# Where an RWKV step prepares its second unit and scales its output, and which loads an attention phase issues first

## The chip, the cores and the metric

The kernel runs on one core of a Trainium2 chip, as one program with one launch. The metric is device time in microseconds (us), the median of several runs; lower is better. The engines are TensorE (PE, with its weight loads PEld), VectorE (DVE), ScalarE (ACT), GpSimd (POOL) and SyncE (SP), which issues nearly all DMAs. Each engine takes its instructions in the order in which the program lists them, and waits at the first one whose inputs or buffers are not ready.

## The reference

One hybrid layer over 2048 tokens of width 1024, in float32. Cut to what matters here:

```python
p = rmsnorm(x, norm_g) @ w_in                  # 3076 columns, split into the parts below
# RWKV branch, 8 heads of 64, a recurrence over tokens:
S = S*w_t + sa*(kk_t*a_t) + v_t*k_t            # sa = S @ (-kk_t)
y = S @ r_t
y = (y - mean)*rsqrt(var + 64e-5)*gn_g + gn_b  # per head
y = y + sum(r*k*r_k)*v;  y = y*silu(gate)
# attention branch, 8 heads: every query picks its best 256 keys by an index score,
# softmax over them, then o * silu(gate)
out = rmsnorm(x + concat(y_rwkv, y_attn) @ w_out, final_g)
```

## The kernel before, in words

There are four phases. `phase_as` makes the projections and, for each of the 16 blocks of 128 queries, a mask of the chosen keys (`d_mask`). `phase_r` is the RWKV recurrence. `phase_t` is the attention with those masks, in 64 units: a unit (p, b) is head pair p of 4 and query block b of 16, with b the inner loop, so a unit costs more the larger b is. `phase_w` is the output product, one block of 128 tokens at a time; a block needs the RWKV output and all four head pairs' attention output of its tokens.

The phases are not run one after the other. A planner orders each engine's instructions ahead of time, on a timeline of its own. Among the instructions that are ready on this timeline the one with the lowest priority number goes first. Numbers rise in the order in which the code is written, and `later(n)` adds n millions: RWKV's state chain has no addition, the work around it has one (`e.later()`), attention two, the output product three. So attention fills the places that RWKV leaves. The order that comes out is fixed; on the chip an instruction that is not ready holds up all that stand behind it on its engine. `tc.issue_after(ins)` (in the code also `behind(ins)`) adds that the instructions of a block which run on the engine of `ins` stand behind it.

`phase_r` takes 16 steps n of 128 tokens. Each step has two units (i = 0, 1; each holds two of the four pairs of heads) and two chunks of 64 tokens (o = 0, 1). The functions:

- `prep(n, i)` loads a unit (`ld`, two buffers), makes decays, keys and the matrix `E` on DVE, ACT and PE, and `bv`. It ends with a scaling of `BK` on POOL, which stands behind the last instruction of the inverse that was traced before it (`scaled_after`).
- `systems` sends four pieces of `E` to memory (`du`, L1015) and reads them back spread over 128 partitions as `A` (L1017). `A` has one buffer, so its read can only start when the inverse before has read the last of the old `A`.
- `inverse` is 62 small POOL instructions in a row (L1031, L1033); its result goes out as `dx` (L1034) and comes back as `TT` (four DMAs, L1038).
- `prep2` transposes a unit's keys and values.
- `chain(n, o)` runs one chunk through the state: products, a solve with `TT` in two halves (first `TT` product L1068), and the new state `S` by two adds on DVE (L1096). What it returns as `state` is the last of them.
- `tail_norm` makes mean and variance of a step's output `y` on DVE and ACT, the power -0.5 on POOL (`gst`, L1112, behind the inverse's last instruction) and the scaling of `y` on DVE (L1113). `tail_out` transposes `y`, applies gains, `bv` and the gate (POOL, L1128 and L1129), and stores it.

At step n the code opens with inverse(n+1), then `tail_norm` of step n-1 with the scaling as its last instruction, then prep(n+2, 0) behind the last state. After chain(n, 0) come `prep2` of step n+1, prep(n+2, 1) behind the state of chain(n, 0), and `systems` for n+2. After chain(n, 1) comes `tail_out` of step n-1.

In `phase_t`, `load(p, b)` issues a unit's DMAs on SP: keys `kt` and values every fourth unit, queries `q` every second, mask `mk` and gate `ga` always. The first unit is loaded ahead of the loop; in turn i the loop loads unit i+1.

Of the kernel before, what the change touches and what calls it, by code (L numbers as in the profile page):

```python
# [14 lines left out]
OP = mybir.AluOpType  # L15
# [871 lines left out]
def phase_r(env):  # L887


    e = NS(env)  # L890
    nc, tc, pa, ps, dma, V, S, G, PE, f32, rpow, nm, ident = (
        e.nc, e.tc, e.pr, e.psr, e.dma, e.V, e.S, e.G, e.PE, e.f32, e.rpow, e.nm, e.ident)
# [3 lines left out]
    NU = 2 * NC  # L896
# [203 lines left out]
    def tail_norm(y):  # L1100

        yv = y.rearrange("t c (h i) -> t (c h) i", h=2)
        st = tl([128, 3, NU], F32, "gst", 2)
        V.tensor_reduce(st[:, 0], yv, axis=AX.X, op=OP.add)
        V.tensor_scalar(st[:, 0], st[:, 0], 1.0 / 64, None, op0=OP.mult)
        bc = lambda a: a[:, :, None].to_broadcast([128, NU, 64])
        V.tensor_tensor(yv, yv, bc(st[:, 0]), op=OP.subtract)
        sq = tl([128, NU, 64], F32, "ysq")
        S.activation(sq, yv, AF.Square)
        V.tensor_reduce(st[:, 1], sq, axis=AX.X, op=OP.add)  # L1110
        V.tensor_scalar(st[:, 1], st[:, 1], 1.0 / 64, 64e-5, op0=OP.mult, op1=OP.add)
        m = G.tensor_tensor(st[:, 2], st[:, 1], e.mhalf[:, :NU], op=OP.pow)  # L1112
        V.tensor_tensor(yv, yv, bc(st[:, 2]), op=OP.mult)  # L1113
        return m.ins

    def tail_out(us, y):

# [20 lines left out]
    def behind(ins):  # L1138
        return tc.issue_after(ins) if ins else ExitStack()
# [7 lines left out]
    first = G.memset(eLs[0][:, :, 0:1], 1.0).ins  # L1147
# [10 lines left out]
    y0, b0, state = None, None, None  # L1158
    for n in range(N):
        b = batch.pop(n)  # L1160
        new = batch[n + 2] = begin(n + 2) if n + 2 < N else None
        nx = batch.get(n + 1)
        with e.later():
            if nx:
                nx.TT, first = inverse(nx.A)
            if b0:
                with behind(first):
                    tail_norm(y0)
            if new:
                with behind(state):  # L1170
                    new.us.append(prep(n + 2, 0, new.eC, first))
        y = tl([128, NC, 128], F32, "y", 2)
        state = chain(b.us, b.TT, b.eC, y, n, 0)
        with e.later():
            if nx:
                for u in nx.us:
                    prep2(u)
            if new:
                with behind(state):
                    new.us.append(prep(n + 2, 1, new.eC, first))  # L1180
                new.A = systems(new.us)
        state = chain(b.us, b.TT, b.eC, y, n, 1)
        with e.later():
            if b0:
                tail_out(b0.us, y0)
        y0, b0 = y, b
    with e.later():
        tail_norm(y0)
        tail_out(b0.us, y0)


def phase_t(env):

    e = NS(env)
# [124 lines left out]

    units = [(p, b) for p in range(NP) for b in range(NB)]  # L1320
    last, stores, marks = None, [], {}
    load(*units[0])
    for i, u in enumerate(units + [None]):
        out = []
        ready, stores = stores, []
        if i + 1 < len(units):
            with tc.issue_after(load(*units[i + 1])):
                for x in ready:
                    dma(*x)
        else:  # L1330
            for x in ready:
                dma(*x)
        parts = [scores(*u, out)] if u else []
        if last:
            parts.append(attend(*last))
        while parts:
            parts = [g for g in parts if next(g, parts) is not parts]
        last = (*u, *out) if u else None
# [81 lines left out]
```

## Time and profile before

| | us |
|---|---|
| median of three runs (lowest, highest) | 2103.36 (2098.55, 2105.53) |
| the profiled execution, device time | 2104.7 |
| its span, first to last instruction | 2102.9 |
| PE busy in the span | 1803.3 (86%) |
| DVE, ACT, POOL busy | 1296.7, 1019.8, 795.3 |

The mean granted TensorE clock of the execution is 0.906 of full speed. RWKV's loads begin at 981 us; until then the span belongs to `phase_as`. The inverses run from 1025 to 1731 us, RWKV's last output is made at about 1800 us, and the last attention product ends at 2045 us. A busy share is an average over a stage; which wait ends last in a stage is read from the waits and the timeline.

### The profile page before, as it was taken

Reading aid. Unit: us, or ns where it says so; the run is one execution under the profiler, and the core shown is the slowest. Engines: PE = TensorE matmul, PEld = TensorE weight load, DVE = VectorE, ACT = ScalarE, POOL = GpSimd, SP = SyncE. Lnnn points to the kernel's source line nnn. Section 1 sums busy time; section 2 is a strip of 40 time slices with the busy share of each in tenths; the row PEclk is TensorE's granted clock in tenths of the full one; section 3 lists DMA queues with packets and bytes.
Section 4 is the critical chain, followed back from the end, with each engine's and each line's share of the span. In section 5 each row is a group of like instructions: output and inputs, shape, how many; then the busy total and the mean of one; then the engine's idle time right before and its main releaser. Section 6 shows DMA issues by size and latency. Waiting matters only on the chain.

```text
span 2102.9 us, 36153 instructions
## 1 busy us (share of the span) xinstructions
PE 1803.3 (86%) x12906; PEld 1421.8 (68%) x12906; DVE 1296.7 (62%) x3050; ACT 1019.8 (48%) x1966; POOL 795.3 (38%) x1925
## 2 busy tenths in 40 slices
PE   5788998879796988986788988886988889899998
PEld 4666877658575867765566766665766667587776
DVE  5532538979779698986656557564756654644432
ACT  4422494453444744441355555454655567643431
POOL 1110124353544354562445645654546650100000
PEclk9778999989798999998799998798988899999999
DMA  7526334332262434234844355343454324744223
GB/s 248 199 94 200 108 101 135 101 115 85 75 239 63 135 107 136 91 95 125 204 102 105 95 136 147 105 119 98 115 143 131 93 78 108 233 128 128 66 93 112
DMA packets 309038, 262.50 MB, mean 125 GB/s; under 512 B 82544, under 2 KB 258288, under 8 KB 307696
## 3 DMA queue, kind: packets, MB, share of 16 engines
q1 hardware_dynamic: 304464, 248.03, 40.1%
q0 software_dynamic: 4384, 12.06, 1.8%
q8 instruction: 104, 1.70, 0.4%
q14 instruction: 86, 0.70, 0.1%
HBM read 166.37 MB, written 97.85 MB: 126 GB/s over the span
## 4 chain that ended last, share of the span: by engine, by line
PE 23%; POOL 14%; DMA 12%; issue 5%; DVE 4%; SPq 1%; ACT 1%; POOLq 0%; DVEq 0%; ACTq 0%
DMA A<-du 6%; POOL Xr L1033 6%; POOL Xtmp L1031 5%; PE om L1304 3%; PE po L1381 3%; PE po L1382 3%; PE po L1384 3%; PE tr L1295 3%; DMA dx<-Xr 2%; PE s L1261 2%; PE s L1262 1%; DMA TT<-dx 1%; DMA ld<-d_rw 1%; POOL yo L1129 1%; POOL gst L1112 1%
## 5 line engine op out<-in xcount | busy, mean ns | idle before, releaser
L577 PE MATMUL pm<-xh,wh 128*128 128x512 f32 x800 | 330.4, 414 | 20.3 <-DVE t L588 11.8
L578 PE MATMUL pm<-xl,wh 128*128 128x512 f32 x800 | 327.0, 409 | 0.0
L579 PE MATMUL pm<-xh,wl 128*128 128x512 f32 x800 | 326.1, 408 | 0.0
L1263 DVE CUSTOM_DVE_ANT_0 sc<-s,mk 128x512 f32<-128x512 f32 (+3 forms) x320 | 187.9, 607 | 102.8 <-PE s L1262 76.0
L1297 ACT ACTIVATE pt<-tr 128x512 f32<-128x512 f32 (+1 forms) x288 | 157.9, 569 | 160.8 <-PE tr L1295 115.9
L1031 POOL TENSOR_TENSOR Xtmp<-Xr,A 128x60 f32<-128x60 f32 (+24 forms) x496 | 146.9, 296 | 225.8 <-DMA A<-du 181.8
L577 PEld LDWEIGHTS pm<-xh,wh 128*128 128x128 f32 x800 | 158.1, 198 | 61.7 <-DVE t L588 13.7
L1270 ACT ACTIVATE sc<-sc,mx 128x128 f32<-128x128 f32 (+15 forms) x128 | 153.0, 1198 | 63.0 <-DVE mx L1269 62.7
L1295 PE MATMUL tr<-ident,sc 128*128 128x128 f32 x1088 | 180.1, 292 | 3.0 <-ACT pt L1297 2.6
L579 PEld LDWEIGHTS pm<-xh,wl 128*128 128x128 f32 x800 | 157.3, 197 | 36.4
L578 PEld LDWEIGHTS pm<-xl,wh 128*128 128x128 f32 x800 | 158.0, 197 | 35.4
L1304 PE MATMUL om<-pt,vt 128*64 128x128 f32 x2176 | 174.0, 295 | 6.2 <-DVE ga L1287 6.2
L1261 PE MATMUL s<-kt,q 128*128 128x512 f32 (+2 forms) x320 | 144.2, 454 | 35.8 <-DVE mx L1263 32.2
L1033 POOL TENSOR_TENSOR Xr<-Xr,Xtmp 128x60 f32<-128x60 f32 (+24 forms) x496 | 151.3, 305 | 37.4
L1304 PEld LDWEIGHTS om<-pt,vt 128*64 128x64 f32 x2176 | 134.2, 146 | 37.6 <-issue 19.6
L1295 PEld LDWEIGHTS tr<-ident,sc 128*128 128x128 f32 x1088 | 133.5, 149 | 33.9 <-issue 11.4
L317 ACT ACTIVATE mk<-x,st 128x1920 bf16<-128x1920 f16 (+5 forms) x72 | 98.0, 1361 | 103.6 <-POOL st L314 103.6
L249 ACT ACTIVATE rl<-lg,wi 128x512 f32<-128x512 f32 (+3 forms) x152 | 94.0, 631 | 99.6 <-PE lg L247 53.1
L1262 PE MATMUL s<-kt,q 128*128 128x512 f32 (+2 forms) x320 | 123.3, 389 | 8.1 <-DMA q<-d_q 8.0
L320 DVE TENSOR_SCALAR_CACHE_REDUCE mk<-x,st 128x2048 bf16<-128x2048 f16 (+5 forms) x72 | 120.6, 1675 | 1.4
L254 DVE SCALAR_TENSOR_TENSOR xs<-rl,wi,xs 128x512 f32<-128x512 f32 (+3 forms) x108 | 73.5, 681 | 60.9 <-ACT rl L249 60.1
L1387 POOL TENSOR_TENSOR st<-st 128x1 f32<-128x1 f32 x16 | 3.1, 195 | 277.1 <-ACT po L1386 277.1
(329 smaller groups left out, 3937.7 us busy)
## 6 DMA issues: line engine op xcount, KB each, us to landing
wraw<-in_w_in_dram SPq DMA_DIRECT2D x42, 512.0 KB
d_rw<-t SPq DMA_DIRECT2D x80, 256.0 KB
ld<-d_rw SPq DMA_DIRECT2D x32, 640.0 KB
q<-d_q SPq DMA_DIRECT2D x128, 128.0 KB
d_q<-t SPq DMA_DIRECT2D x32, 256.0 KB
d_kt<-t SPq DMA_DIRECT2D x32, 256.0 KB
kt<-d_kt SPq DMA_DIRECT2D x32, 256.0 KB
A<-du SPq DMA_DIRECT2D x16, 512.0 KB
```

What stands on the lines that cost most here:

```text
L577: PE.matmul(pm, wh[:, k], XH[g][:, k], start=k == 0, stop=False)
L578: PE.matmul(pm, wh[:, k], XL[g][:, k], start=False, stop=False)
L579: PE.matmul(pm, wl[:, k], XH[g][:, k], start=False, stop=k == KD - 1)
L1031: G.tensor_tensor(tmp[:, :m, :w], Xr[:, :m, s:s + 1].to_broadcast([128, m, w]), A[:, s:s + 1, s + 1:].to_broadcast([128, m, w]), op=OP.mult)
L1033: m_ = G.tensor_tensor(Xr[:, :m, s + 1:], Xr[:, :m, s + 1:], tmp[:, :m, :w], op=OP.add)
L1261: PE.matmul(pS[:, :wp], qh[:, h, qs], k[:, h, :wp], start=True, stop=False)
L1262: PE.matmul(pS[:, :wp], ql[:, h, qs], k[:, h, :wp], start=False, stop=True)
L1263: V.tensor_tensor_reduce(out=rows[h][:, c0:c0 + w], in0=pS[:, :w], in1=mk[:, c0:c0 + w], scale=1.0, scalar=LOW, op0=OP.add, op1=OP.max, ac ...
L1270: marks[p, b] = S.activation(rows[h][:, :n], rows[h][:, :n], AF.Exp, bias=mx[:, h, 4:5], accum_out=sums[:, h:h + 1]).ins
L1295: PE.transpose(pt[:, i, h], rows[h][:, (kb + i) * 128:(kb + i) * 128 + 128], ident)
L1297: S.activation(w[:, :m], pt[:, :m], AF.Copy)
L1304: PE.matmul(po[HALF[h]], v[:, (kb + i) % 4, HALF[h]], w[:, i, h], start=kb + i == 0, stop=kb + i == b)
```

## The change

`prep` of both units and `systems` for step n+2 move to the opening of step n. `tail_norm` ends with the power and returns the scaling of `y`, which is traced after chain(n, 0) and behind its state. In `phase_t` the first three units are loaded before the loop, at a priority one million ahead of everything without an addition; the loop's loads begin with the fourth unit.

```diff
         V.tensor_scalar(st[:, 1], st[:, 1], 1.0 / 64, 64e-5, op0=OP.mult, op1=OP.add)
-        m = G.tensor_tensor(st[:, 2], st[:, 1], e.mhalf[:, :NU], op=OP.pow)
-        V.tensor_tensor(yv, yv, bc(st[:, 2]), op=OP.mult)
-        return m.ins
+        rpow(st[:, 2], st[:, 1])
+        return lambda: V.tensor_tensor(yv, yv, bc(st[:, 2]), op=OP.mult)
...
             if b0:
                 with behind(first):
-                    tail_norm(y0)
+                    scale = tail_norm(y0)
             if new:
-                with behind(state):
-                    new.us.append(prep(n + 2, 0, new.eC, first))
+                for i in range(2):
+                    with behind(state):
+                        new.us.append(prep(n + 2, i, new.eC, first))
+                new.A = systems(new.us)
         y = tl([128, NC, 128], F32, "y", 2)
         state = chain(b.us, b.TT, b.eC, y, n, 0)
         with e.later():
+            if b0:
+                with behind(state):
+                    scale()
             if nx:
                 for u in nx.us:
                     prep2(u)
-            if new:
-                with behind(state):
-                    new.us.append(prep(n + 2, 1, new.eC, first))
-                new.A = systems(new.us)
         state = chain(b.us, b.TT, b.eC, y, n, 1)
...
-        tail_norm(y0)
+        tail_norm(y0)()
         tail_out(b0.us, y0)
...
-    load(*units[0])
+    with e.later(-3):
+        for u in units[:3]:
+            load(*u)
     for i, u in enumerate(units + [None]):
         out = []
         ready, stores = stores, []
-        if i + 1 < len(units):
+        if 3 <= i + 1 < len(units):
             with tc.issue_after(load(*units[i + 1])):
```

`rpow` (L130) is the same POOL power as before, written as a helper.

## Rows read from the trace of the kernel before

**Rows 1.** Stretches: us, busy (count) of PE, PEld, DVE, ACT, POOL; clock, DMA, GB/s.
```profile
979.00:997.40 18.40, 3.91 (x25) 2.79 (x24) 13.53 (x40) 3.40 (x8) 4.03 (x17) 0.59 0.96 243
1025.00:1800.00 775.00, 660.15 (x7439) 511.48 (x7441) 448.22 (x1407) 431.30 (x989) 411.30 (x1177) 0.89 0.45 117
1800.00:1900.00 100.00, 90.55 (x568) 71.60 (x568) 49.37 (x128) 47.62 (x93) 3.26 (x10) 0.95 0.54 172
```

**Rows 2.** Waits of PE, 1025 to 1800 us: us in total, times, longest.
```profile
PE s L1261 <- DVE mx L1263: 32.2, 15, 7.0
PE ch L1068 <- DMA TT<-dx: 29.0, 5, 8.4
PE ch L1051 <- DVE S L1096: 14.4, 1, 14.4
PE rp L982 <- DVE E L977: 11.6, 2, 6.7
PE s L1262 <- DMA q<-d_q: 8.0, 1, 8.0
PE ch L1120 <- DVE S L1096: 7.8, 2, 4.3
PE rp L1051 <- DVE E L977: 4.8, 1, 4.8
...
PE rp L996 <- DVE bv L984: 4.4, 3, 1.7
```

**Rows 3.** Waits of DVE, the same stretch.
```profile
DVE y L1113 <- POOL gst L1112: 74.0, 11, 15.6
```

**Rows 4.** Timeline of DVE in one step: start, us, instruction, idle before and releaser.
```profile
1225.43 1.52 DVE L1113 TENSOR_TENSOR y<-y,gst 128x512 f32<-128x512 f32 x1 [5.60 <-POOL gst L1112]
...
1232.78 1.29 DVE L977 TENSOR_TENSOR E<-rp,mask 128x512 f32<-128x512 f32 x2 [1.38 <-PE rp L974]
```

**Rows 5.** Timeline of PE: two of its waits behind DVE.
```profile
1138.26 0.79 PE L1261 MATMUL s<-kt,q 128*128 128x512 f32 x1 [7.00 <-DVE mx L1263]
...
1733.63 0.58 PE L1261 MATMUL s<-kt,q 128*128 128x256 f32 x1 [6.75 <-DVE mx L1263]
```

**Rows 6.** Timeline of POOL: end of one inverse to start of the next, twice.
```profile
1223.74 1.66 POOL L1112 TENSOR_TENSOR gst<-gst,mhalf 128x8 f32<-128x8 f32 x1
...
1250.71 0.24 POOL L1031 TENSOR_TENSOR Xtmp<-Xr,A 128x31 f32<-128x31 f32 x1 [16.65 <-DMA A<-du]
...
1322.82 1.66 POOL L1112 TENSOR_TENSOR gst<-gst,mhalf 128x8 f32<-128x8 f32 x1
...
1338.06 0.24 POOL L1031 TENSOR_TENSOR Xtmp<-Xr,A 128x31 f32<-128x31 f32 x1 [7.98 <-DMA A<-du]
```

**Rows 7.** Timeline of SP's issues in the same two turns.
```profile
1237.71 0.55 SPq L1017 DMA_DIRECT2D A<-du  x1
...
1325.86 0.83 SPq L1017 DMA_DIRECT2D A<-du  x1
1327.69 1.89 SPq L1038 DMA_DIRECT2D TT<-dx  x4
```

**Rows 8.** Turns with A issued early (first, last, their sum of four), then ten others' sum.
```profile
1322.90:1363.40 40.50, 33.23 (x340) 26.90 (x338) 23.52 (x66) 17.93 (x43) 26.35 (x75) 0.75 0.41 106
...
1644.30:1687.30 43.00, 34.64 (x389) 26.93 (x388) 24.55 (x77) 24.09 (x53) 25.94 (x75) 0.88 0.39 101
sum 168.30, PE 135.67 PEld 108.06 DVE 97.36 ACT 85.83 POOL 104.39; mean PE 33.92 PEld 27.01 DVE 24.34 ACT 21.46 POOL 26.10
...
sum 471.30, PE 407.06 PEld 314.30 DVE 281.38 ACT 268.71 POOL 253.21; mean PE 40.71 PEld 31.43 DVE 28.14 ACT 26.87 POOL 25.32
```

**Rows 9.** Chain of waits that ended last: start, us, what.
```profile
1608.81 10.17 DMA TT<-dx
```

**Rows 10.** Timeline of SP's issues at the start of RWKV and attention.
```profile
981.01 0.58 SPq L937 DMA_DIRECT2D ld<-d_rw  x1
...
988.03 1.26 SPq L1221 DMA_DIRECT2D kt<-d_kt  x2
```

## Prediction

> **What bounds the kernel now.** I read the stretches first. From 1025 to 1800 us, while RWKV and attention share the core, PE is busy 660 of 775 us, so 115 us are idle, at a mean granted clock of 0.89; from 1800 on, attention and the output product keep PE at 90% and more [rows 1]. What is not done beside RWKV is done behind it, on a PE that is nearly full. So PE's work is the bound, and a change is worth what it takes from PE's idle and slow time between 979 and 1800 us; RWKV ending earlier is worth nothing by itself.
>
> Next the waits. PE's long ones in that stretch end with DVE (attention's maxima, E, the state S) or with TT [rows 2], and DVE's own longest wait is one instruction: the scaling of y, 74.0 us in 11 waits for the power on POOL [rows 3]. The power stands behind the 62 instructions of the inverse. One step shows the ring: the inverse ends at 1223.74, DVE comes free of the scaling only at 1227 after 5.60 us idle, E of unit 1, queued behind it, is made at 1232.78 [rows 4], so A is issued at 1237.71 [rows 7] and the next inverse starts at 1250.71, 27.0 us after the end of the one before [rows 6]. Where E was ready in time, A is issued at 1325.86, 3.0 us after the inverse's end [rows 7], and the gap is 15.2 us [rows 6]. Of the 14 turns from 1091 to 1730.6 us, end of inverse to end of inverse, I call four early in this sense (A issued before TT) and ten late. A late turn takes 471.3/10 = 47.1 us with 6.4 us of PE idle, an early one 168.3/4 = 42.1 us with 8.2 us [rows 8].
>
> **The change part by part.** The number of instructions stays: prep, systems, power and scaling run as often as before, on the same tiles. Only places in the queues change.
>
> *Both units at the opening.* E of unit 1 no longer stands behind the scaling, so A waits for the last inverse alone and late turns become as short as early ones: 10 x (47.1 - 42.1) = 50 us off RWKV. This is no gain of time yet; it is in PE's waits that the gain must show. Of these, S 14.4 and 7.8, E 11.6 and 4.8, and four of the waits for the maxima, 7.00 the first and 6.75 the last [rows 5], 21.9 together, end just after DVE's scaling: 60.5 us, of which 52.7 in late turns and 7.8 in early ones [rows 2]. The scaling itself still waits for its power: I count 14 of the 16 scalings as standing behind the state of chain(n, 0) already, so its new place changes their order little, and what helps is that the inverse ends sooner relative to DVE. If late turns keep as much of it as early ones do (7.8/4 = 1.95 us), 52.7 - 19.5 = 33 us go; if all goes, 52.7. I take 43, the middle, since the 14.4 us wait is one of the two scalings that the new order does move behind the state.
>
> *A goes out before TT.* With du ready, A's read (512 KB) is issued at once after dx, and TT's four DMAs follow it [rows 7]. TT then takes 10.17 us [rows 9]. Queued behind it on PE is the solve of the next chain, and behind that whatever attention follows in the order. In the early turns PE waited for TT (29.0 - 8.4)/4 = 5.15 us each (the 8.4 belongs to the turn before 1091), in the ten late ones not at all [rows 2]. Bounds for the ten: 0 and 51.5 us. I take 31, above the middle, since every early turn shows this wait, though their attention units are small and the large ones of other turns give PE more to do before the solve.
>
> The Trainium skill, page "DMA: Bandwidth & Descriptors", section "Queues, rings and completion order", says that each DMA engine takes the descriptors of one ring in order. By that a TT issued after A starts behind A's descriptors in every turn, as the 10.17 us in [rows 9] agree with; the sum with the whole of 10.17 in ten turns instead of 31 would be 71 us higher. It speaks against the change, and stands beside the rival on the slower side.
>
> *What else moves with unit 1.* Its loads ld and vt, four du and A are issued half a step sooner; SP meets A's wait for the inverse where it already waits for dx, so behind it stand TT and attention's loads as now. Its bv needs a buffer that POOL frees by yo, behind the first instructions of an inverse that waits for A. DVE holds PE up for 4.4 us by this today [rows 2]; with unit 1 sooner between 0 and twice, so +0 to +4.4, and I take +2.
>
> *Three units loaded ahead.* SP issues RWKV's first load at 981.01 and attention's first at 988.03 [rows 10]; PE idles 14.5 of the 18.4 us from 979 [rows 1] and 8.0 us later for q of a further unit [rows 2]. If the loads go out before 981, up to 22 us could be filled, but the three units are the smallest and the next ones still load behind RWKV. If they go out at 981, RWKV's loads come later by their issue time, an estimate of 10 us for 17 DMAs at about 0.6 us (the ld's issue time in the same rows), with little else to run. Bounds -22 and +10; I take -6, the gap of about 7 us between the two issues in [rows 10], which is the nearest.
>
> *More attention left for later.* RWKV is some 50 us shorter; PE is 9.5% idle in 1800 to 1900 us [rows 1], so what is left over loses 0 to 5 us more there. I take +2.
>
> The sum: -43 + 31 + 2 - 6 + 2 = -14 us on the profiled execution's 2104.7, so 2090.7. That execution is 1.3 us above the median of the runs, so I say 2089.
>
> **The rivals.**
>
> 1. *The fill stays and TT doesn't matter.* Attention beside RWKV is as much per turn as now, PE has always something to do until TT is there, and all of the 52.7 goes: -52.7 + 2 - 6 = -57, 2047 us. For it: TT is waited for in no late turn. Against it: a shorter turn in the planner's order also holds less attention.
>
> 2. *Nothing changes in the order.* The planner places by readiness on its own timeline; if unit 1 came no sooner there (DVE and PE taken), the ring stays: only the start, -6 + 2, about 2099 us. For it: the scaling stands where the change puts it in 14 of 16 steps. Against: E of unit 1 no longer waits for chain(n, 0).
>
> 3. *Slower: all turns become like the early ones.* The planner shortens its turn as much as the chip does, or more, and puts less attention into each; the chip's turn can't fall under inverse plus A's read, about 42 us, and PE waits for TT and for the scaling instead. PE idle rises by 8.2 - 6.4 = 1.8 us in ten turns: +18. The clock falls with it: in the early turns 0.75 to 0.88, mean 0.825 (0.79 and 0.88 the two between) [rows 8], so PE spends about 2 x 0.175 x 42.1 = 14.7 us of a turn at the lower level (1.2 GHz), 6.5 of them working, which loses 3.3 us. The same sum over 775 us at 0.89 gives 28 us, 1.6 a turn [rows 1]. Ten times 1.7: +17. Together 18 + 17 + 2 - 6 + 2 = +33, about 2136 us. The point from which it decides: attention work per turn falling by more than about 5 us while the turn stays at 42. For it: early turns hold 33.9 us of busy PE, late ones 40.7. Against it: two of the four early turns lie where attention's units are smallest, so their thin fill may be those units' own.
>
> **How the numbers follow.** Forecast 0.38, its own range 2070 to 2102; rival 1 0.13; rival 2 0.18; rival 3 0.31. A measurement of this kernel tells a change of 0.3%, 6.3 us, from none. Faster by more: rival 1 and 0.33 of the forecast's 0.38, with 0.02 of rival 2, 0.48. Within: 0.05 of the forecast, 0.14 of rival 2 and 0.01 of rival 3, 0.20. Slower: the rest, 0.32. The range reaches from rival 1 almost to rival 3's price: 2045 to 2130.
>
> **What would show it.** Right: A issued within about 3 us of each inverse's end, gaps of 15 to 18 us in the POOL timeline, turns near 42 us, DVE's wait for the power well under 74 us, PE's wait for TT up to about 60 us, and the last attention product before 2045 us. Wrong in the gain: PE idle and the clock from 1025 to RWKV's end no better per turn than 7 us and 0.89, with more attention behind RWKV. Wrong in the ring: A issued later than TT as now. At the start: PE's first attention product before 997 us with RWKV's first inverse still near 1025. A slower RWKV start, or waits for TT of 10 us in most turns, would make the prediction wrong on the side of rival 3.

## Result and profile after

| | before | changed |
|---|---|---|
| median of 11 runs each, side by side (us) | 2102.34 | 2113.08 |
| profiled execution's span | 2102.9 | 2112.2 |
| PE busy in it | 1803.3 | 1811.1 |
| mean granted TensorE clock | 0.906 | 0.908 |

The ratio is 1.0054, 95% interval 1.0043 to 1.0066: some 11 us slower, where I had said 14 us faster. The start did what it was to do, RWKV's ring did not, and PE's lost time moved from one part of a turn to another and grew.

The same three stretches of the changed kernel as in [rows 1] (us, busy (count) of PE, PEld, DVE, ACT, POOL; clock, DMA share, GB/s):

```profile
979.00:997.40 18.40, 10.82 (x33) 7.02 (x34) 7.32 (x41) 5.59 (x21) 2.74 (x15) 0.55 0.98 248
1025.00:1800.00 775.00, 648.69 (x7338) 508.12 (x7337) 452.37 (x1355) 419.86 (x956) 418.88 (x1168) 0.89 0.46 114
1800.00:1900.00 100.00, 90.18 (x563) 70.16 (x559) 55.50 (x156) 53.99 (x115) 10.10 (x18) 0.95 0.60 187
```

PE starts with attention 7 us fuller, but beside RWKV it is busy 648.7 us in place of 660.2 at the same mean clock. What was not done there is done at the end: the last attention product ends at 2054 us, 2045 before.

PE's waits from 1025 to 1800 us in the changed kernel, as in [rows 2]:

```profile
PE tr L1295 <- ACT pt L1297: 20.1, 5, 11.3
PE rp L1051 <- DVE E L977: 16.9, 2, 9.4
PE rp L982 <- DVE E L977: 14.0, 6, 9.3
PE om L1304 <- DVE ga L1287: 11.2, 3, 10.6
PE s L1261 <- DVE mx L1263: 10.6, 12, 3.1
PE rp L974 <- DVE bv L984: 9.0, 3, 4.7
PE ch L1068 <- DMA TT<-dx: 6.9, 2, 6.4
...
PE rp L996 <- DVE bv L984: 3.5, 1, 3.5
```

The waits for S and two thirds of those for the maxima are gone, and those for TT fell from 29.0 to 6.9 us. In their place stand E, bv and attention's own pt and ga. DVE's waits of the same stretch, as in [rows 3]: the scaling's grew from 74.0 to 85.3 us.

```profile
DVE y L1113 <- POOL gst L130: 85.3, 13, 10.7
...
DVE bv L984 <- POOL yo L1127: 20.6, 5, 6.4
```

One turn of the changed kernel, whose inverse ends at 1454.2 us: first DVE's E and scaling, as in [rows 4], then SP's issues, as in [rows 7], then POOL's first instruction of the next inverse, as in [rows 6].

```profile
1438.90 1.26 DVE L977 TENSOR_TENSOR E<-rp,mask 128x512 f32<-128x512 f32 x2
...
1446.94 1.28 DVE L977 TENSOR_TENSOR E<-rp,mask 128x512 f32<-128x512 f32 x2
...
1455.83 1.52 DVE L1113 TENSOR_TENSOR y<-y,gst 128x512 f32<-128x512 f32 x1 [4.65 <-POOL gst L130]
```
```profile
1454.22 0.58 SPq L1034 DMA_DIRECT2D dx<-Xr  x1
1459.03 1.79 SPq L1038 DMA_DIRECT2D TT<-dx  x4
1460.92 0.89 SPq L1015 DMA_DIRECT2D du<-E  x2
1461.90 0.55 SPq L937 DMA_DIRECT2D ld<-d_rw  x1
1463.12 0.56 SPq L1017 DMA_DIRECT2D A<-du  x1
```
```profile
1475.24 0.24 POOL L1031 TENSOR_TENSOR Xtmp<-Xr,A 128x31 f32<-128x31 f32 x1 [14.34 <-DMA A<-du]
```

Here E of both units is made 6 us before the inverse ends, as I had wanted. But in SP's order du of unit 1 stands behind dx and TT, and A behind du, so A goes out 8.9 us after the inverse's end and the next inverse starts 21.0 us after it. Over the 13 turns from 1133.3 to 1748.0 us, both units' E are ready before the inverse's end in eight (in a ninth 0.4 us after it); A goes out at once in one of the eight, in the other seven 6.7 to 14.1 us later. The mean from inverse's end to A is 8.4 us (before: 8.1), and only one turn has A ahead of TT (before: four). The 13 turns together:

```profile
sum 614.76, PE 511.47 PEld 399.96 DVE 364.58 ACT 332.02 POOL 349.85; mean PE 39.34 PEld 30.77 DVE 28.04 ACT 25.54 POOL 26.91
```

47.3 us a turn; before, the same 13 turns took 45.9 us each (the 14 of [rows 8] 45.7). At the start the first load of RWKV goes out at 989.07 us (981.01 in [rows 10]) and the first inverse starts at 1036.00 (1024.96 before), since 17 of attention's DMAs now stand ahead of it:

```profile
989.07 0.57 SPq L937 DMA_DIRECT2D ld<-d_rw  x1
```

### The profile page after: what moved, and what is told of

Read it like the earlier page. It is cut to its first block, busy times and chain, and to the rows that moved or that the text cites. A ratio compares the mean times of both kernels' runs of the same rounds, so it can differ in the third digit from the quotient of the medians.

```text
span 2112.2 us, 36165 instructions
## 1 busy us (share of the span) xinstructions
PE 1811.1 (86%) x12906; PEld 1431.4 (68%) x12906; DVE 1311.5 (62%) x3050; ACT 1020.2 (48%) x1966; POOL 809.9 (38%) x1925
## 4 chain that ended last, share of the span: by engine, by line
PE 23%; POOL 14%; DMA 11%; issue 4%; DVE 4%; SPq 1%; ACT 1%; POOLq 0%; ACTq 0%; DVEq 0%
POOL Xr L1033 6%; POOL Xtmp L1031 6%; DMA A<-du 6%; PE om L1304 4%; DMA dx<-Xr 3%; PE tr L1295 3%; PE po L1386 3%; PE po L1383 3%; PE po L1384 3%; PE s L1261 2%; PE s L1262 1%; PE rp L974 1%; DMA ld<-d_rw 1%; SPq L1038 1%; POOL yo L1128 0%
## 5 line engine op out<-in xcount | busy, mean ns | idle before, releaser
L1031 POOL TENSOR_TENSOR Xtmp<-Xr,A 128x60 f32<-128x60 f32 (+24 forms) x496 | 152.9, 308 | 228.0 <-DMA A<-du 191.8
L577 PEld LDWEIGHTS pm<-xh,wh 128*128 128x128 f32 x800 | 157.7, 197 | 59.1 <-DVE t L588 13.3
L1304 PE MATMUL om<-pt,vt 128*64 128x128 f32 x2176 | 172.8, 296 | 17.8 <-DVE ga L1287 12.2
L1033 POOL TENSOR_TENSOR Xr<-Xr,Xtmp 128x60 f32<-128x60 f32 (+24 forms) x496 | 156.9, 316 | 37.4
L1261 PE MATMUL s<-kt,q 128*128 128x512 f32 (+2 forms) x320 | 149.1, 469 | 24.1 <-DVE mx L1263 11.1
L249 ACT ACTIVATE rl<-lg,wi 128x512 f32<-128x512 f32 (+3 forms) x152 | 94.0, 631 | 99.2 <-PE lg L247 45.9
L1262 PE MATMUL s<-kt,q 128*128 128x512 f32 (+2 forms) x320 | 126.7, 399 | 0.6 <-DMA q<-d_q 0.6
```

Source lines behind the costliest of these rows:

```text
L577: PE.matmul(pm, wh[:, k], XH[g][:, k], start=k == 0, stop=False)
L1031: G.tensor_tensor(tmp[:, :m, :w], Xr[:, :m, s:s + 1].to_broadcast([128, m, w]), A[:, s:s + 1, s + 1:].to_broadcast([128, m, w]), op=OP.mult)
L1033: m_ = G.tensor_tensor(Xr[:, :m, s + 1:], Xr[:, :m, s + 1:], tmp[:, :m, :w], op=OP.add)
L1261: PE.matmul(pS[:, :wp], qh[:, h, qs], k[:, h, :wp], start=True, stop=False)
L1262: PE.matmul(pS[:, :wp], ql[:, h, qs], k[:, h, :wp], start=False, stop=True)
L1304: PE.matmul(po[HALF[h]], v[:, (kb + i) % 4, HALF[h]], w[:, i, h], start=kb + i == 0, stop=kb + i == b)
```

## The experiments

Times of one plan spread by some 8 us to either side of its median, so each kernel was run five rounds or more against the kernel before, and verdicts rest on the ratios. A profile is one execution of these.

### One part at a time

**The three loads alone.**

```diff
-    load(*units[0])
+    with e.later(-3):
+        for u in units[:3]:
+            load(*u)
...
-        if i + 1 < len(units):
+        if 3 <= i + 1 < len(units):
```

> The kernel before with the three attention units loaded ahead and nothing else of the change. Theory L (the early loads delay RWKV's first load by about 8 us, 981 to 989 us as in the kernel after, and this is the loss): slower than before by 6 to 12 us, ratio 1.003 to 1.006, first inverse near 1036 us. Theory R (the loss is in the ring of inverse, du and A: no early turns left because SP issues unit 1's du behind dx and TT): the loads fill PE by some 10 us at the start and cost RWKV about as much, ratio 0.998 to 1.002, four or so early turns left.

2085.2 us, ratio 0.9919 (0.9899 to 0.9939): 17 us faster. Theory L is dead: the first inverse does start at 1037 us, 12 us late, and the kernel gains all the same. Theory R leaves the loss to the ring, but had set the gain of the loads at nothing.

**The preparation alone.**

```diff
             if new:
-                with behind(state):
-                    new.us.append(prep(n + 2, 0, new.eC, first))
+                for i in range(2):
+                    with behind(state):
+                        new.us.append(prep(n + 2, i, new.eC, first))
+                new.A = systems(new.us)
```

> The kernel before with both units prepared at the opening, the scaling and the loads as before. Theory R: the planned order on SP puts A before TT in two turns (four before), so two turns of about 5 us longer and little else: ratio 1.002 to 1.006, DVE's wait for the power 70 to 90 us. Theory L: without the early loads no loss, ratio 0.997 to 1.001, first inverse near 1025 us.

2136.3 us, ratio 1.0170 (1.0147 to 1.0192): 36 us slower, far more than two turns of 5 us can cost. DVE's wait for the power is 99.7 us.

**The scaling half a step later, alone.**

```diff
-        m = G.tensor_tensor(st[:, 2], st[:, 1], e.mhalf[:, :NU], op=OP.pow)
-        V.tensor_tensor(yv, yv, bc(st[:, 2]), op=OP.mult)
-        return m.ins
+        rpow(st[:, 2], st[:, 1])
+        return lambda: V.tensor_tensor(yv, yv, bc(st[:, 2]), op=OP.mult)
...
+            if b0:
+                with behind(state):
+                    scale()
```

> The kernel before with the scaling of y half a step later and nothing else. My prediction said that its place changes little, since 14 of 16 scalings stand behind that state already: ratio 0.998 to 1.002, DVE's wait for the power within 10 us of 74. A rival S (the later scaling makes yo and the store of y late, which holds SP and POOL): ratio 1.003 to 1.006.

2108.4 us, ratio 1.0045 (1.0027 to 1.0064): 9 us slower, rival S's size. The wait for the power is 85.1 us.

**The change without the loads** (preparation and scaling; against the changed kernel).

```diff
-    with e.later(-3):
-        for u in units[:3]:
-            load(*u)
+    load(*units[0])
```

> The changed kernel without the three early loads: both units at the opening and the scaling later. Theory L: the loss is gone, ratio to before 0.997 to 1.001, first inverse near 1025 us. Theory R: the loss stays, ratio 1.003 to 1.007, at most two turns with A issued before TT, mean turn 47 us.

2132.3 us, ratio 1.0146 (1.0123 to 1.0169). Beside the preparation alone (1.0170) the later scaling costs nothing that can be told. The loads give back 1.0146 - 1.0054 = 0.9%, as they gave 0.8% alone. Theory L falls a second time.

**The change without the preparation** (scaling and loads; against the changed kernel).

```diff
-                for i in range(2):
-                    with behind(state):
-                        new.us.append(prep(n + 2, i, new.eC, first))
-                new.A = systems(new.us)
+                with behind(state):
+                    new.us.append(prep(n + 2, 0, new.eC, first))
...
+            if new:
+                with behind(state):
+                    new.us.append(prep(n + 2, 1, new.eC, first))
+                new.A = systems(new.us)
```

> The changed kernel with the preparation of unit 1 and systems put back to half a step later: the scaling later and the three early loads stay. If the parts add up (scaling 1.0045, loads 0.992 of before, preparation the rest), this is 0.994 to 0.999 of before, and the preparation is what makes the changed kernel slow. Rival I (the parts act through one order made ahead and don't add): outside that, above 1.001.

2093.5 us, ratio 0.9967 (0.9949 to 0.9984); the sum of the parts would be 0.9919 x 1.0045 = 0.9964. So the preparation is what makes the changed kernel slow: 1.0054 - 0.9967 = 0.9%, 18 us. This kernel and the changed one differ in nothing else, and I use the two to see where that goes.

### Where the preparation loses it

I cut each of 13 turns (end of inverse to end of inverse) at 20 us and let the trace sum up the parts. First the first 20 us of the 13 turns, then the rest of them: kernel before, change without the preparation, changed kernel.

```profile
sum 260.00, PE 195.68 PEld 148.77 DVE 170.11 ACT 127.49 POOL 78.34; mean PE 15.05 PEld 11.44 DVE 13.09 ACT 9.81 POOL 6.03
...
sum 336.21, PE 306.79 PEld 241.62 DVE 180.44 ACT 203.01 POOL 258.28; mean PE 23.60 PEld 18.59 DVE 13.88 ACT 15.62 POOL 19.87
```
```profile
sum 260.00, PE 200.91 PEld 155.76 DVE 172.40 ACT 127.92 POOL 79.73; mean PE 15.45 PEld 11.98 DVE 13.26 ACT 9.84 POOL 6.13
...
sum 327.59, PE 299.82 PEld 236.94 DVE 189.97 ACT 207.02 POOL 255.36; mean PE 23.06 PEld 18.23 DVE 14.61 ACT 15.92 POOL 19.64
```
```profile
sum 260.00, PE 212.87 PEld 170.60 DVE 117.15 ACT 146.51 POOL 68.40; mean PE 16.37 PEld 13.12 DVE 9.01 ACT 11.27 POOL 5.26
...
sum 354.76, PE 298.59 PEld 229.35 DVE 247.44 ACT 185.51 POOL 281.45; mean PE 22.97 PEld 17.64 DVE 19.03 ACT 14.27 POOL 21.65
```

PE's idle time is the stretch less its PE; its clock loss is, row by row, busy time x (1 - clock), summed over the 13 rows behind each line:

| 13 turns, us | first 20: idle, clock loss | rest: idle, clock loss |
|---|---|---|
| before | 64.3, 34.9 | 29.4, 21.2 |
| change without preparation | 59.1, 40.4 | 27.8, 2.7 |
| changed | 47.1, 31.5 | 56.2, 24.0 |

The gain that I forecast is there: in the first 20 us of the turns, where DVE stands at the scaling, PE loses 20.9 us less with the preparation (59.1 + 40.4 against 47.1 + 31.5). It is more than given back in the rest: 49.7 us more. DVE says why: 55 us of its work (172.4 to 117.2) leave the front of the turns and 57 us (190.0 to 247.4) turn up in the rest. The preparation's own DVE instructions (lines 950 to 984) are most of this: 65 to 28 us in the front, 100 to 140 us in the rest. Unit 1's preparation used to run where PE stood idle anyhow; now it runs where PE was full, 30.5 us lost of 327.6. (The 13 turns net 28.8 us; the two profiled executions differ by 17.2. The changed kernel's 13 turns are 27 us longer, and outside them it loses about 12 us less.) Against the kernel before, the changed one loses 20.6 us less in the front and 29.6 us more in the rest, 9.0 us together; the two spans differ by 9.3.

Two more pairs of kernels differ in the preparation alone, and show the same. From the kernel before to the preparation alone PE's loss goes from 99 to 81 us in the front and from 51 to 90 us in the rest; from the scaling alone to the change without the loads, from 113 to 74 us and from 41 to 95 us. In the three pairs 37 to 40 us of the preparation's DVE work leave the front, and the rest has 40 to 51 us more of it.

Three turns' rest without the preparation, and three of the changed kernel:

```profile
1168.94:1195.71 26.77, 24.89 (x322) 19.70 (x322) 17.25 (x54) 18.45 (x36) 22.08 (x67) 1.00 0.32 84
1215.71:1245.09 29.38, 27.00 (x368) 21.29 (x366) 15.45 (x50) 20.14 (x44) 21.16 (x67) 1.00 0.58 154
...
1711.41:1736.53 25.12, 25.12 (x326) 19.71 (x327) 10.94 (x36) 18.35 (x33) 20.23 (x67) 1.00 0.19 53
```
```profile
1153.25:1179.83 26.58, 18.98 (x230) 14.45 (x228) 18.68 (x51) 13.11 (x27) 22.19 (x65) 0.98 0.34 97
...
1522.24:1555.95 33.71, 27.61 (x261) 20.42 (x255) 20.99 (x66) 14.71 (x43) 21.38 (x67) 0.77 0.57 138
...
1627.34:1653.56 26.22, 22.47 (x192) 17.54 (x188) 20.82 (x57) 9.77 (x22) 21.83 (x65) 0.67 0.28 78
```

Without the preparation the rest of a turn runs at the full clock nearly throughout (0.95 to 1.00 in all 13); with it PE stops again in that part, five of 13 turns run it at 0.67 to 0.89, and the stops lie apart from the one at the inverse's end. What PE waits for there differs: in the changed kernel 18 us of its waits end with the preparation's E, BK and bv (0.3 without the preparation early), in the change without the loads 20 us end with attention's maxima (1.8 in the scaling alone). PE's products of a preparation take longer as a group too (both kernels, 1000 to 1800 us; the changed kernel first): PE is busy with them for 9 us more, though a single one takes no longer.

```profile
L974 PE MATMUL rp<-X,BK 64*128 64x128 f32 x506 | 62.3, 309 | 12.1 <-DVE bv L984 9.0 <-DVE BK L965 2.7 <-DVE BK L964 0.3
```
```profile
L974 PE MATMUL rp<-X,BK 64*128 64x128 f32 x512 | 53.0, 310 | 11.6 <-DVE BK L964 11.6
```

### Which part of the preparation

**prep early, du and A as before.**

```diff
             if new:
-                with behind(state):
-                    new.us.append(prep(n + 2, 0, new.eC, first))
+                for i in range(2):
+                    with behind(state):
+                        new.us.append(prep(n + 2, i, new.eC, first))
...
             if new:
-                with behind(state):
-                    new.us.append(prep(n + 2, 1, new.eC, first))
                 new.A = systems(new.us)
```

> The kernel before with both units' prep at the opening, but systems (du and A) traced half a step later as before; no early loads, scaling as before. It splits the 36 us that the whole move cost. Theory R (A's and du's place in SP's queue is what costs): ratio 1.000 to 1.007. Rival C (the cost is in prep of unit 1 itself: its DVE, ACT and PE work crowds the opening of the step, where tail_norm and the E of unit 0 are, and attention's chains on DVE come late): ratio 1.012 to 1.020, close to the 1.017 of the whole move.

2133.1 us, ratio 1.0168 (1.0132 to 1.0204): the whole of it, so the two preps cost it and the early `systems` adds nothing. On theory R it says less than I had hoped: A goes out 8.7 us after an inverse's end here and in the preparation alone, ahead of TT in the same turns, so A's place in the order didn't change between the two. What speaks against R is the kernel with 6 buffers for bv (below): its A goes out 13.7 us after an inverse's end, and it is 0.5% faster than the kernel before. The order of du and A on SP explains why the ring didn't get shorter; as the cause of a loss of 18 to 36 us it doesn't fit that kernel.

**du on ScalarE's queue** (in the changed kernel, L1015).

```diff
-                dma(du[i, k].rearrange("u s t -> s u t"),
+                S.dma_start(du[i, k].rearrange("u s t -> s u t"),
```

> The changed kernel with the four du pieces of each step issued by ScalarE's queue in place of SP's, so that du of unit 1 no longer stands behind dx, TT and attention's loads on SP. Theory R (the loss of 31 us that both units at the opening cost comes from A going out late, because SP holds du up): A is issued some 3 to 6 us sooner after an inverse's end (10 us in the changed kernel), gaps of 16 to 18 us (21), and at least a third of the 31 us comes back: ratio to before 0.988 to 0.999. Rival P (the length of a turn doesn't set the time; what counts is how often PE stops long enough for its clock to fall, in an order made ahead): gaps may shrink, but the time stays within 0.4% of the changed kernel, ratio 1.001 to 1.010.

2117.3 us, ratio 1.0081 (1.0049 to 1.0114), rival P's range. The gaps didn't shrink: A goes out 9.7 us after an inverse's end on average, still behind TT on SP. Three issues of one turn, whose inverse ends at 1425.2 us:

```profile
1425.27 0.58 SPq L1034 DMA_DIRECT2D dx<-Xr  x1
1430.04 1.81 SPq L1038 DMA_DIRECT2D TT<-dx  x4
1437.36 0.57 SPq L1017 DMA_DIRECT2D A<-du  x1
```

So it doesn't tell what an early A would be worth.

**The pair half a step later** (three loads ahead, both preps and `systems` after the first chunk).

```diff
-            if new:
-                with behind(state):
-                    new.us.append(prep(n + 2, 0, new.eC, first))
...
             if new:
-                with behind(state):
-                    new.us.append(prep(n + 2, 1, new.eC, first))
+                for i in range(2):
+                    with behind(state):
+                        new.us.append(prep(n + 2, i, new.eC, first))
                 new.A = systems(new.us)
```

> The kernel before with the three early loads, and the prep of both units half a step later, after the first chunk, in place of one at the opening and one there. Theory C1 (crowding: two preps in one half of a step leave PE waiting at each of their handoffs with DVE, wherever the pair stands): slower than the early loads alone by 20 us or more, ratio to before 1.001 to 1.015 (loads alone 0.992). Rival C2 (the opening is the wrong place, since there the pair meets the stand at the scaling and the inverse): about as fast as the early loads alone, ratio 0.988 to 0.997.

2108.7 us, ratio 1.0054 (1.0035 to 1.0073); against the loads alone 1.0054 - 0.9919 = 1.35%, 28 us. The time lies in the range of crowding (C1), and not in that of the opening as such (C2). Its profiled execution was 13 us faster than its median, so I take no sizes from its trace.

### Taking waits away

**The power not behind the inverse** (the changed kernel; then the loads alone with the same edit).

```diff
-                with behind(first):
-                    scale = tail_norm(y0)
+                scale = tail_norm(y0)
```

> The changed kernel with the power of tail_norm no longer placed behind the inverse's last instruction; POOL takes it where the planner finds it ready, among the inverse's instructions too. Theory S, that of my prediction (DVE's stand at the scaling, 85.3 us in 13 waits in the changed kernel, is what holds PE up through what is queued behind it on DVE): the wait falls below 40 us and 15 to 40 us come off: ratio to before 0.985 to 0.998. Rival P: the wait falls as much, but PE's idle time turns up behind other releasers (E, pt, ga), and the time stays within 0.4% of the changed kernel: ratio 1.001 to 1.010.

> The kernel before with the three early loads and the power of tail_norm not placed behind the inverse's last instruction. Theory S (DVE's stand at the scaling is what still costs, 89.0 us in 13 waits with the early loads): 5 to 30 us faster than the loads alone, ratio to before 0.978 to 0.990. Rival P (as in the changed kernel, where the same edit brought nothing): ratio 0.991 to 1.000.

2121.8 us, 1.0108 (1.0073 to 1.0142), and 2118.6 us, 1.0104 (1.0077 to 1.0132): both slower than their parents. But DVE's wait for the power hardly fell in the one (row of the changed kernel with this edit; 85.3 us without) and rose in the other (106.8 us; 89.0 without):

```profile
DVE y L1113 <- POOL gst L130: 76.8, 13, 10.6
```

The wait moved instead. In the changed kernel DVE comes free of nearly every such wait 1.6 us after an inverse's end; with this edit nine of eleven waits over 1 us end 35 us or more after it, and in the loads alone with the same edit all twelve 27 to 41 us after it. PE's loss moved too: 28 and 60 us less in the first 20 us of the turns, 38 and 90 us more in the rest. So what the wait itself is worth was not tried; but both runs agree with the table: a stand of DVE in the rest of a turn goes with more loss than one in its front.

**Two buffers for A; 12 buffers for bv in the changed kernel; 12 with the loads alone; one unit each half step, earlier.**

```diff
-        A = tl([128, 32, 32], F32, "A")
+        A = tl([128, 32, 32], F32, "A", 2)
```
```diff
-        u.bv = tl([128, 2, W], F32, "bv", 8)
+        u.bv = tl([128, 2, W], F32, "bv", 12)
```
```diff
-        u.vt = tl([128, 2, C + W], F32, "vt", 4)
+        u.vt = tl([128, 2, C + W], F32, "vt", 5)
...
             if new:
                 with behind(state):
-                    new.us.append(prep(n + 2, 0, new.eC, first))
+                    new.us.append(prep(n + 2, 1, new.eC, first))
+                new.A = systems(new.us)
...
+            if n + 3 < N:
+                b3 = batch[n + 3] = begin(n + 3)
                 with behind(state):
-                    new.us.append(prep(n + 2, 1, new.eC, first))
-                new.A = systems(new.us)
+                    b3.us.append(prep(n + 3, 0, b3.eC, first))
```

The third diff also gives X 7 buffers, BK 5, E 7 and eC 5, prepares unit 0 of step 2 ahead of the loop, and loads two units ahead. The four in the order of the heading:

> The changed kernel with two buffers for A, so that its read needn't wait for the last instruction of the inverse before. Theory R: A is read during the inverse before, gaps of 5 to 15 us in place of 21, RWKV's last inverse ends 60 us or more sooner than 1748 us, and the time falls, ratio 0.98 to 0.995. Rival P: the gaps shrink, and the time stays within 0.5% of the changed kernel or gets longer, since PE then meets TT and the scaling with less attention planned in each turn: ratio 1.000 to 1.012.

> The changed kernel with 12 buffers for bv in place of 8, so that unit 1's bv needn't wait for POOL's yo of an older step (DVE waited 20.6 us for it in five places, PE 12.5 us behind bv). Theory B (this wait is a part of what the early prep costs): bv's waits go, and 5 to 15 us come off: ratio to before 0.998 to 1.003. Rival P (PE's idle time only moves to another releaser): the time within 0.3% of the changed kernel, ratio 1.002 to 1.009.

> The kernel before with the three early loads and 12 buffers for bv in place of 8. Theory T (the few buffers of RWKV's tiles are what keeps its steps apart on the planner's timeline, and what leaves attention its room in each step): as in the changed kernel with 12, RWKV's turns get short, below 42 us, PE loses 20 us or more of each, and the time is 5% or more above before. Rival U (in this order unit 1's bv comes half a step later, so the number of its buffers binds nothing): turns of 45 us as with 8, ratio 0.988 to 0.996.

> The kernel before with two attention units loaded ahead, and the preparation half a step earlier without crowding: at the opening of step n unit 1 of step n+2 and systems, after its first chunk unit 0 of step n+3; one more buffer each of vt, X, BK, E and eC. Theory C1 (what costs is that two units are prepared in one half of a step): as two loads alone or a little faster, ratio to before 0.980 to 0.992, turns of 42 to 45 us. Theory T (a unit ready sooner shortens RWKV's turn in the planned order, and each turn then holds less attention than PE could do): turns under 42 us, ratio above 1.01. That readiness itself is worth what my prediction said would be 0.97 to 0.98.

2333.2, 2367.1, 2374.3 and 2378.1 us; ratios 1.1115, 1.1284, 1.1302 and 1.1337, each known to 0.4%. Turns fall to 36 to 40 us, and I first read that as theory T. The trace says something else. Of the kernel with two buffers for A: POOL's last output of RWKV and what follows it, SP's first load of attention, PE's first attention product.

```profile
1614.73 1.41 POOL L1128 TENSOR_TENSOR yo<-yo,gr 128x256 f32<-128x256 f32 x2
1616.09 0.43 POOL L1209 TENSOR_SCALAR_AFFINE_SELECT sel<-sel 4x256 f32<-4x256 f32 x1
```
```profile
1616.58 1.29 SPq L1221 DMA_DIRECT2D kt<-d_kt  x2
```
```profile
1623.70 0.80 PE L1261 MATMUL s<-kt,q 128*128 128x256 f32 x2 [11.34 <-DMA q<-d_q]
```

Attention doesn't start until RWKV is over, in all four (first load at 1616.6, 1651.4, 1664.2, 1662.9 us; 988 before). RWKV has PE to itself and can't fill it (1025 to 1600 us of this kernel):

```profile
1025.00:1600.00 575.00, 394.84 (x4312) 308.16 (x4311) 271.42 (x594) 182.22 (x464) 404.16 (x1148) 0.61 0.31 77
```

The four edits add 4 to 9.5 KB per partition by their tile shapes, and even a constant of attention's (`sel`) waits for RWKV's end, so the likely reason is that both phases' tiles no longer fit side by side; that was argued, not tested. The four runs answer none of their questions. They show what the overlap is worth: without it RWKV's last output comes some 137 to 184 us sooner and the kernel takes 235 to 280 us longer.

**6 buffers for bv, with the loads alone.**

```diff
-        u.bv = tl([128, 2, W], F32, "bv", 8)
+        u.bv = tl([128, 2, W], F32, "bv", 6)
```

> The kernel before with the three early loads and 6 buffers for bv in place of 8, so that a step's bv waits for the output of the step three before. Theory T: turns get longer than 45 us, up to 50, with more attention in each, and the time is that of 8 buffers or up to 1% less: ratio 0.982 to 0.993. Rival V (a longer turn adds stops of PE behind bv, and RWKV ends so late that the output product waits for it): ratio 0.997 to 1.02.

2090.8 us, ratio 0.9952 (0.9934 to 0.9969), between the two ranges: turns of 48.2 us (45.3 with 8), and about 7 us slower than the loads alone. Longer turns by themselves cost little, and so does an A that goes out 13.7 us after an inverse's end (8.5 with 8 buffers).

### The loads

**One unit ahead; two ahead** (the kernel before; the diff is that of two).

```diff
-    load(*units[0])
+    with e.later(-3):
+        for u in units[:2]:
+            load(*u)
...
-        if i + 1 < len(units):
+        if 2 <= i + 1 < len(units):
```

> The kernel before with only the first attention unit loaded at the early priority; the loop loads the second and third as before. If the gain of the loads (17 us for three units) comes from PE filled at the start, 979 to 1025 us (9.3 us more busy there with three units), one unit gives a part of it: ratio 0.994 to 0.999. If it comes from a different order over the whole of RWKV (fewer stops of PE at the low clock, 16 in place of 22), one unit may give anything: outside 0.994 to 0.999, with the number of low-clock spells following the time at some 3 us each.

> The kernel before with two attention units loaded ahead, between one (0.9988 of before) and three (0.992). If the gain is PE work fetched to the start, it lies between them, 0.992 to 0.998. If it is another order over all of RWKV, it can lie outside, and PE's low-clock spells (21 with one, 16 with three) say where.

2093.4 us, 0.9988 (0.9971 to 1.0005), and 2076.3 us, 0.9892 (0.9870 to 0.9915). Two units bring as much as three or more (the intervals overlap), outside the range for work fetched to the start. It has the lowest ratio of all the kernels: 23 us below before and 34 below the changed one. Its stretches (start, RWKV), then RWKV's first load:

```profile
979.00:1025.00 46.00, 37.69 (x221) 27.43 (x222) 33.96 (x119) 19.25 (x58) 2.28 (x3) 0.71 1.02 229
1025.00:1800.00 775.00, 662.63 (x7580) 513.53 (x7582) 466.42 (x1445) 447.38 (x1021) 411.99 (x1177) 0.91 0.48 125
```
```profile
982.25 0.56 SPq L937 DMA_DIRECT2D ld<-d_rw  x1
```

RWKV's loads are 1 us later than before (8 with three units in the changed kernel), and PE is busy 37.7 us of the first 46 (24.2 before). Beside RWKV it is busy 2.5 us more than before, at a clock of 0.91 in place of 0.89.

**Two units ahead in the changed kernel.**

```diff
-        for u in units[:3]:
+        for u in units[:2]:
...
-        if 3 <= i + 1 < len(units):
+        if 2 <= i + 1 < len(units):
```

> The changed kernel with two attention units loaded ahead in place of three. If the parts add up (preparation 1.0087, scaling 1.0045, two loads 0.9892), ratio to before 0.998 to 1.006. Rival I (the order made ahead reacts to each edit by itself, and two loads are good in one order and not in the other): above 1.008 or below 0.996.

2120.3 us, ratio 1.0117 (1.0090 to 1.0145): rival I. Two loads are level with three or better in one order and lose to three in the other (1.0117 against 1.0054); so a part of these gains belongs to the order that comes out, and not to the loads.

## Why the prediction was wrong

- *The bound*: held. The time follows what PE loses, idle and by its clock, beside RWKV: from 980 to 1800 us (stretches of 5 us) 178 us with two loads ahead, 204 before and 222 with the preparation alone, at spans of 2067.6, 2102.9 and 2134.4 us. Over the 16 kernels in which the two phases run side by side, this loss and the span have a correlation of 0.97. It doesn't tell all: the changed kernel loses 206 us there, 2 more than before, and its span is 9.3 us longer.
- *Both units at the opening, -43*: the step that failed, in the clause "A waits for the last inverse alone and late turns become as short as early ones". Alone the edit costs 36 us, undone from the changed kernel 18. E of unit 1 does come earlier, ahead of the scaling in nine of 13 turns, but A doesn't, because du and TT stand ahead of it on SP; turns got 1.4 us longer. And I asked only which of PE's waits would go, not where the moved DVE work would land: the gain at the front (20.9 us) was real, and the rest of the turns lost 49.7. (One reading behind the 43 was off as well, without weight for the outcome: the 6.75 us wait at 1733.63 lies behind the last turn, which ends at 1730.6, so 46 and not 52.7 us lie in late turns.)
- *The scaling itself, no cost*: held in company with the preparation; alone it costs 9 us, and beside the loads 10 (0.9967 against 0.9919).
- *A before TT, +31*: didn't happen. One turn has that order, and PE's wait for TT fell by 22 us. What it would have cost can be read elsewhere: over 13 turns of each of the 20 kernels, TT, which needs dx, goes out 10.9 to 12.2 us after dx in the 32 turns in which A went out just ahead of dx, and 4.7 to 8.8 us after it in all others. The rule of the Trainium skill, page "DMA: Bandwidth & Descriptors", section "Queues, rings and completion order", which I weighed there, that each DMA engine takes the descriptors of one ring in order, agrees with this.
- *bv, +2*: PE's waits behind bv went from 4.4 to 12.5 us, +8.
- *Three loads, -6*: mis-sized; -17 alone and -19 in the changed kernel, though RWKV starts 11 us later, where I had set that at most +10 against the gain. The gain is more than the gap at the start that I priced; part of it belongs to the order that came out.
- *More attention left, +2*: it stood on an RWKV some 50 us shorter; the last inverse ends 17 us later (1748.0 and 1730.6). PE is as idle from 1800 to 1900 us as before (9.8 and 9.5 us), and its last attention product ends 9 us later.
- *The rivals*: rival 3 had the side, with a mechanism that didn't occur (short turns). Its floor of 42 us for a turn doesn't hold: turns take 38 to 40 us in the three kernels without overlap that keep one buffer for A. Its sum over the clock was too small: 28 us from 1025 to 1800 us in the kernel before, against 62 counted below. Rival 2 had the ring unchanged, and called that harmless.

So the sum's parts that I can size are: preparation +18, scaling and loads together -7 (0.9967), +11 in all, as measured. How the 18 divide between the lost cover at the front and the new stops in the rest is the table's to say; what in the planner's order puts unit 1 into the second part of the turn stays open, as does what a truly early A would bring beside attention.

## What to carry to other kernels

Before moving work off a waiting engine, cut the loop's turn into parts and look at where the bound engine is full: work that was done while it stood idle was free, and an earlier place can be dearer than a late one. A wait named in the trace is not a saving; ask what will stand there next, and whether a queue in between (here SP's) keeps the old order. Change one part at a time: here the loads gave 17 us alone, half of what the preparation cost alone, and hid it.

## What the runs showed of the hardware

In these traces PE's clock falls after a stop, and the work that follows pays for it. In the changed kernel (1525 to 1547 us), 5 us in which PE is busy for 2.93 are followed by 7 us at a clock of 0.52, that is at the lower level of 1.2 GHz nearly throughout, with PE busy 6.50 of them, and then by full speed:

```profile
1525.00:1530.00 5.00, 2.93 (x34) 2.00 (x30) 4.92 (x19) 3.24 (x10) 0.00 (x0) 1.00 0.44 91
1530.00:1537.00 7.00, 6.50 (x45) 4.63 (x45) 3.56 (x13) 1.97 (x6) 5.64 (x18) 0.52 0.63 169
1537.00:1547.00 10.00, 8.53 (x99) 6.03 (x97) 5.08 (x14) 5.64 (x16) 8.04 (x26) 1.00 0.61 175
```

Counted in stretches of 1 us from 1025 to 1800 us, the kernel before has 22 such spells (stretches in a row with a clock under 0.75) and loses 62 us there by its clock (busy time x (1 - clock)), the loads alone 16 and 46, the preparation alone 25 and 77, the change without the preparation 17 and 49: 2.8 to 3.1 us each in all four. So the loss goes with the number of spells and not with the idle time: the preparation alone has only 5 us more idle time than before in that stretch and 15 us more clock loss, and the change without the preparation has 8 us more idle time and 13 us less clock loss.

A DMA that is issued behind a large read on the same queue lands late. With 12 buffers for bv in the changed kernel, A (512 KB) goes out ahead of dx in eight of 13 turns, and TT, which waits for dx, follows dx after 10.9 to 12.0 us; in the five turns with dx ahead of A it follows after 4.7. One of the eight (its inverse ends at 1111.4 us):

```profile
1111.12 0.55 SPq L1017 DMA_DIRECT2D A<-du  x1
1111.72 0.56 SPq L1034 DMA_DIRECT2D dx<-Xr  x1
1122.95 1.79 SPq L1038 DMA_DIRECT2D TT<-dx  x4
```

So an A that goes out ahead of dx is not free: it makes the inverse's own result about 7 us later.

POOL's inverse gets slower when DVE prepares units beside it. Its instructions with the preparation, then without (1091 to 1800 us; busy, mean ns):

```profile
L1033 POOL TENSOR_TENSOR Xr<-Xr,Xtmp 128x60 f32<-128x60 f32 (+24 forms) x441 | 140.1, 318 | 33.1
L1031 POOL TENSOR_TENSOR Xtmp<-Xr,A 128x60 f32<-128x60 f32 (+24 forms) x440 | 136.2, 310 | 203.6 <-DMA A<-du 171.7
```
```profile
L1033 POOL TENSOR_TENSOR Xr<-Xr,Xtmp 128x60 f32<-128x60 f32 (+24 forms) x447 | 137.4, 307 | 33.3
L1031 POOL TENSOR_TENSOR Xtmp<-Xr,A 128x60 f32<-128x60 f32 (+24 forms) x446 | 131.5, 295 | 209.4 <-DMA A<-du 176.9
```

11 and 15 ns more, 31 times each: 0.8 us of each turn. Within the changed kernel, an instruction of the inverse that runs beside DVE's preparation takes 71 ns longer on average than one of the same shape with DVE idle, and one beside other DVE work 29 ns (272 and 282 of them). The Trainium skill, page "SBUF — State Buffer", section "SBUF: two separate sides", says that DVE and GpSimd share one pair of ports, and that a DVE instruction with two inputs in SBUF and a GpSimd instruction that reads SBUF hold it one at a time, each for its whole length; these numbers agree in direction.
